# Three modulation sets of the first block, each for one vector, summed by elements on VectorE instead of multiplied on TensorE

## The chip, the cores and the metric

The kernel runs on one core of a Trainium2 chip. The metric is the time of one execution on the device in microseconds; before the change the median of three runs is 2258.77 us (2258.53 to 2259.44). The engines that matter here are TensorE (PE in the profile: matrix products and transposes), VectorE (DVE), ScalarE (ACT), GpSimd (POOL) and SyncE (SP), whose queue starts the loads of the weights by DMA.

## The reference

The program is a chain of three blocks on 256 tokens of width 1024, all in fp32: a block of attention, spatial gating and a mixture of experts; a block with a half feed-forward layer before and after a two-way recurrent mixing; and a last block. The change touches the first one, which in short is:

```python
def adaln(cvec, w_mod, b_mod):
    m = jax.nn.silu(cvec) @ w_mod + b_mod
    return jnp.split(m, 6, axis=-1)

def modulate(x, g, shift, scale):
    return rmsnorm(x, g) * (1 + scale) + shift

sh1, sc1, gt1, sh2, sc2, gt2 = [m[:, None, :] for m in adaln(c, w_mod, b_mod)]
csh1, csc1, cgt1, csh2, csc2, cgt2 = adaln(c_ctx, w_mod, b_mod)
hl = modulate(xl, g_mix, sh1, sc1)
hc = modulate(xc, g_mix, csh1, csc1)
...
xl_new = xl + gt1 * (mix_l @ w_out)
xl_new = xl_new + gt2 * expert_choice_ffn(modulate(xl_new, g_ffn, sh2, sc2), w_router, w1, w3, w2)
```

A modulation set is one of the six slices of 1024 columns of `silu(c) @ w_mod + b_mod`, where `w_mod` has 1024 x 6144 numbers, so a set reads 4 MB. The first two sets (sh1, sc1) are needed for the tokens and for the context (c and c_ctx). As the block returns only the tokens, the sets gt1, sh2 and sc2 are needed for c alone.

## The kernel before

Work on one core is put out in program order for each engine by a scheduler, which interleaves what the code writes as separate steps; the order on an engine is then fixed, and an engine whose next instruction waits does nothing else meanwhile.

*Loads.* Every weight comes in tiles of 1 MB (128 x 2048 fp32) by `load` (L253), in the order in which the code asks for them, through SyncE's queue (L258). The tiles go round a ring of buffers: six in the first block, more later. A load is issued only when the tile that had its buffer before has been used by the engine that reads it.

*Split weights.* For products of the projections a weight tile is split into a high and a low half (`halves`, L269: `wh` by ScalarE, L273, `wl` by VectorE, L274), each from a pool `hl` of five buffers per kind, and a product is three fp32r products (`mm`, L282 to L284: high x high, low x high, high x low).

*Modulation sets by products.* `ada_start` (L391) loads four tiles and does 32 products of the tile with both vectors in 32 columns (L399, tile `pa`; the profile counts 64 passes), then copies the sum out (`adaR`; L243 on ScalarE or L245 on VectorE, taking turns). `ada_end` (L406) transposes it twice on TensorE (L410, `pat`) and VectorE adds the bias (L412) into a column tile of shape 128 x 8 x 2.

*Modulation sets by elements.* `ada_one` (L419) is in the kernel already, for two sets in ffn a. VectorE multiplies each half tile by the vector's value in its partition and adds it up: one TENSOR_SCALAR (L430) and seven SCALAR_TENSOR_TENSOR (L432) of 128 x 1024 into `aacc`, from a pool `scr` of two buffers. Then TensorE adds the 128 partitions in eight products with a column of ones (L435), and VectorE adds the bias (L437).

*The order in `phase_a` (L478).* After the projections of keys, values, queries and of the gating's second half (pv), the set gt1 is started (`ada_start` of set 2), then keys are transposed (L626, `pkt`), the gating's first half u is projected (`pu`, 48 products at L282 to L284), gt1 is ended, sh2 started (set 3), queries are transposed (L638, `pqt`), and sh2 ended. Then come the scores (L689, `pS`), the softmax (L471 to L476: maximum `nm`, exponential `P` on ScalarE, reciprocal `rc`, scaling), the transposes of its result (L700, `pP`) and the values (L707, `pO`), in four pairs of heads; sc2 (set 4) stands around pair 0, a first and a second set of `w_ada` around pairs 1 and 2, with the gating between. Before the output projection (`proj_out`, products `pW`, 96 times L282 to L284, from the four tiles of `w_out`) gt1 is spread over the partitions by `bcast` (L373, `pb`). After the projection the residual is added with gt1 (L769, L770), the norm, sh2 and sc2 give the router's input (L347) and the experts' (L845, `pX`), and the experts' products begin (L874). These read 384 tiles of 1 MB; their first loads stand in SyncE's queue directly behind the last twelve tiles of `w_ada` of the first block.

Of the kernel before, what the change touches and what calls it, by code (L numbers as in the profile page):

```python
# [10 lines left out]
F32 = mybir.dt.float32  # L11
# [218 lines left out]
class Kern:  # L230
# [185 lines left out]
            op=OP.add)  # L416
        return c

    def ada_one(self, w, p, s, bias, name, eng=None):  # L419

        nc = self.nc
        eng = eng or nc.vector
        acc = self.scr.tile([128, 1024], F32, tag="scr", name="aacc")
        for kp in range(4):
            t = self.load(w[p * 4 + kp])
            for i in range(2):
                k = 2 * kp + i
                tk = t[:, i * 1024:(i + 1) * 1024]
                if k == 0:
                    eng.tensor_scalar(acc, tk, s[:, k, 0:1], None, op0=OP.mult)  # L430
                else:
                    eng.scalar_tensor_tensor(acc, tk, s[:, k, 0:1], acc, op0=OP.mult, op1=OP.add)  # L432
        ps = self.psc.tile([128, 512], F32, tag="c", name="pa1")
        for j in range(8):
            nc.tensor.matmul(ps[:, j:j + 1], acc[:, j * 128:(j + 1) * 128], self.ones[:, 0:1], start=True, stop=True)  # L435
        c = self.pers.tile([128, 8, 1], F32, name=name)
        nc.vector.tensor_tensor(c[:, :, 0], ps[:, 0:8], self.col(bias, 8 * p, 8), op=OP.add)  # L437
        return c
# [39 lines left out]
    def phase_a(self, pf_es):  # L478
        tc, nc, a = self.tc, self.nc, self.a
# [11 lines left out]
        def B8(name, dt=F32):  # L491
            return big.tile([128, 2048], dt, tag="b8", name=name)
# [3 lines left out]
        s1 = self.ada_in(("c", "c_ctx"), "s1")  # L496
# [121 lines left out]
        u = mid.tile([128, 2, 512], F32, tag="m4", name="u", bufs=5)  # L618
        for t in range(2):
            nc.scalar.activation(vv[:, t], pv[t], AF.Gelu)  # L620
        gt1R = self.ada_start(a["w_mod"], 2, s1)
        k3f = k3.rearrange("p s h r d -> p s h (r d)")
        for o in range(2):
            ps = self.psc.tile([128, 512], F32, tag="c", name="pkt")
# [1 line left out]
                nc.tensor.transpose(ps[:, s * 128:(s + 1) * 128], k3f[:, s, o], self.ident)  # L626
            self.copy(kz[:, o], ps, "av"[o])
        pu = self.by_token(wu, hl)
        gt1 = self.ada_end(gt1R, 2, "b_mod", "gt1")
        sh2R = self.ada_start(a["w_mod"], 3, s1)  # L630
        for t in range(2):
            nc.scalar.activation(u[:, t], pu[t], AF.Gelu)
        qT = mid.tile([128, 4, 256], F32, tag="m4", name="qT", bufs=5)
        for hh in range(2):
# [3 lines left out]
                    nc.tensor.transpose(ps[:, i * 256 + t * 128:i * 256 + (t + 1) * 128],  # L638
                                        qr[:, t, (2 * hh + i) * 128:(2 * hh + i + 1) * 128], self.ident)
            self.copy(qT[:, 2 * hh:2 * hh + 2], ps.rearrange("p (i n) -> p i n", i=2))  # L640
        sh2 = self.ada_end(sh2R, 3, "b_mod", "sh2")

        for t in range(2):
            sq = self.scr.tile([128, 1024], F32, tag="scr", name="sq")
# [67 lines left out]
        def pair(hp):  # L712
            for i in range(4 * hp, 4 * hp + 4, 2):
                for j in (i + 2, i + 3):
                    if j < 16:
                        scores(j)
                values(i)
                values(i + 1)
# [11 lines left out]

        scores(0)
        scores(1)
        sc2R = self.ada_start(a["w_mod"], 4, s1)
        pair(0)
        sc2 = self.ada_end(sc2R, 4, "b_mod", "sc2")
        R = self.ada_start(a["w_ada"], 0, self.s2)
        pair(1)
        self.m2[0] = self.ada_end(R, 0, "b_ada", "m2_0")
# [1 line left out]
        R = self.ada_start(a["w_ada"], 1, self.s2)  # L740
        pair(2)
        self.m2[1] = self.ada_end(R, 1, "b_ada", "m2_1")
        A2 = self.gain(sc2, self.col("g_ffn"), "A2")
        gt1b = mid.tile([128, 1024], F32, tag="m4", name="gt1b", bufs=5)
        self.bcast(gt1[:, :, 0], 8, gt1b)
        proj_out(2, True, False)
        proj_out(3, False, False)
        pair(3)
        ws = [self.load(a["w_out1"][kp]) for kp in range(2)]
        att.close()  # L750
        with self.more_ring(4, None, last=True):
            proj_out(0, False, False, ws[0])
# [22 lines left out]
        hr = B8("hr").rearrange("p (k n) -> p k n", k=8)  # L775
        self.to_T(xn2, A2[:, :, 0:1], sh2[:, :, 0:1], [hr])
        xs = [B8("xs" + p, F32R).rearrange("p (t d) -> p t d", t=2) for p in "hl"]
# [63 lines left out]
        for k in range(8):  # L841
            ps = self.psc.tile([128, 512], F32, tag="c", name="pX")
            for t in range(2):
                for i in range(2):
                    nc.tensor.matmul(ps, xs[i][:, t, k * 128:(k + 1) * 128], Pm[:, t].rearrange("p e c -> p (e c)"),  # L845
                                     start=(t == 0 and i == 0), stop=(t == 1 and i == 1))
            self.scaled(ps, A2[:, k, 0:1], sh2[:, k, 0:1], [self.xe[:, k]])

# [1096 lines left out]
```

## Time and profile before

| | before |
|---|---|
| median of three runs | 2258.77 us (2258.53 to 2259.44) |
| the profiled execution | 2256.84 us, its span 2255.0 us |
| TensorE busy | 1990.1 us, 88% of the span |
| VectorE busy | 784.2 us, 35% |
| ScalarE busy | 609.9 us, 27% |
| GpSimd busy | 99.8 us, 4% |
| moved by DMA | 666.19 MB, 295 GB/s over the span |
| mean granted TensorE clock | 0.955 |

All durations below come from the one profiled execution, which took 1.93 us less than the median of the runs. Its span runs from the first to the last instruction, and another 1.84 us lie around it. A share of the span is an average over stages that are limited by different things; the slices and the stretches in the section of rows show them apart. In a timeline a row with x16 is a group of 16 of a kind and its duration runs from the first start to the last end; the count is of passes, and one fp32 product can be two or more of them.

### The profile page before, as it was taken

The numbers are of one execution on the slowest core, as the hardware profiler recorded it, in microseconds if no ns is written. First come the engines' busy times: TensorE is split into PE (matmuls) and PEld (weight loads), VectorE is DVE, ScalarE is ACT, GpSimd is POOL, SyncE is SP. The second block draws the span as 40 slices with busy tenths as digits, with TensorE's granted clock in tenths as the row PEclk, the third lists the DMA queues.
The fourth block names the chain that finished last, engine by engine and source line by source line (L and its number), as shares of the span: only waits on it lengthen the run. The fifth ranks groups of instructions, "written<-read, shape, count | busy, mean of one in ns | idle before, by whom it ended". The sixth has DMA issues, their size and how long they took to land.

```text
span 2255.0 us, 29344 instructions
## 1 busy us (share of the span) xinstructions
PE 1990.1 (88%) x12348; PEld 1343.4 (60%) x12348; DVE 784.2 (35%) x1327; ACT 609.9 (27%) x1012; POOL 99.8 (4%) x182
## 2 busy tenths in 40 slices
PE   6998788888877888798887699989999999989997
PEld 4664334444434222243232399989889799978886
DVE  4464000000000000122011366557655555555666
ACT  4342100000000000011000244445444444445564
POOL 2200000000000000000000100010000000021030
PEclk9999899999999999999999999999999999999998
DMA  9669999999999999999999867534135655524221
GB/s 374 254 270 388 420 419 420 419 409 420 420 419 420 420 419 418 420 416 418 420 417 418 353 245 259 182 132 171 54 133 189 244 188 195 186 76 144 100 94 57
DMA packets 93268, 666.19 MB, mean 295 GB/s; under 512 B 10352, under 2 KB 10736, under 8 KB 13392
## 3 DMA queue, kind: packets, MB, share of 16 engines
q1 hardware_dynamic: 92416, 661.99, 74.1%
q8 instruction: 97, 1.59, 0.3%
q0 software_dynamic: 576, 2.10, 0.2%
q10 hardware_dynamic: 144, 0.23, 0.0%
q14 instruction: 35, 0.29, 0.0%
HBM read 663.23 MB, written 1.05 MB: 295 GB/s over the span
## 4 chain that ended last, share of the span: by engine, by line
PE 56%; DMA 25%; issue 10%; DVE 4%; ACT 3%; POOL 1%; SPq 0%; POOLq 0%; DVEq 0%; ACTq 0%
DMA w<-in_w_dram 23%; PE pu L874 7%; PE pu L1092 6%; PE py L912 4%; PE pd L1106 3%; PE pj L284 2%; PE pj L282 2%; PE pj L283 2%; PE pu L282 2%; PE pu L284 2%; PE pu L283 2%; DMA w<-in_w_mod_dram 2%; PE pl L282 1%; PE pl L284 1%; PE pl L283 1%
## 5 line engine op out<-in xcount | busy, mean ns | idle before, releaser
L874 PE MATMUL pu<-w,xe 128*32 128x512 f32 x2048 | 354.2, 668 | 97.4 <-DMA w<-in_w_dram 97.4
L274 DVE TENSOR_TENSOR wl<-w,wh 128x1024 fp32r<-128x1024 f32 (+1 forms) x286 | 348.2, 1221 | 236.2 <-ACT wh L273 236.0
L273 ACT ACTIVATE wh<-w 128x1024 fp32r<-128x1024 f32 (+1 forms) x286 | 299.5, 1053 | 329.0 <-PE pu L283 86.4
L874 PEld LDWEIGHTS pu<-w,xe 128*32 128x32 f32 x2048 | 80.9, 119 | 349.2 <-DMA w<-in_w_dram 187.9
L912 PE MATMUL py<-w,hT 128*32 128x512 f32 x1024 | 181.5, 641 | 65.6 <-DMA w<-in_w_dram 65.6
L283 PE MATMUL pu<-ul,wh 128*128 128x256 f32 x704 | 199.8, 284 | 1.1 <-DVE ul L365 1.1
L282 PE MATMUL pu<-uh,wh 128*128 128x256 f32 x704 | 200.1, 284 | 0.6 <-ACT uh L364 0.5
L284 PE MATMUL pu<-uh,wl 128*128 128x256 f32 x704 | 199.8, 284 | 0.8 <-DVE wl L274 0.8
L1092 PE MATMUL pu<-xu,w 128*128 128x256 f32 x704 | 157.8, 382 | 0.0
L912 PEld LDWEIGHTS py<-w,hT 128*32 128x32 f32 x1024 | 40.4, 115 | 195.5 <-DMA w<-in_w_dram 120.3
L1092 PEld LDWEIGHTS pu<-xu,w 128*128 128x128 f32 x704 | 131.9, 190 | 35.5 <-issue 18.4
L1097 DVE TENSOR_TENSOR xhT<-xs,pu 128x256 f32<-128x256 f32 x22 | 9.3, 421 | 381.6 <-ACT xs L1096 369.5
L283 PEld LDWEIGHTS pu<-ul,wh 128*128 128x128 f32 x704 | 135.6, 193 | 3.0 <-DVE ul L365 1.5
L282 PEld LDWEIGHTS pu<-uh,wh 128*128 128x128 f32 x704 | 135.5, 193 | 2.5 <-ACT uh L364 0.7
L284 PEld LDWEIGHTS pu<-uh,wl 128*128 128x128 f32 x704 | 135.5, 193 | 1.2 <-DVE wl L274 1.2
L1096 ACT ACTIVATE xs<-pu 128x256 f32<-128x256 f32 x22 | 8.4, 383 | 396.7 <-PE pu L1092 396.7
L284 PE MATMUL pj<-mu,wl 128*128 128x256 f32 x320 | 90.9, 285 | 4.4 <-DVE wl L274 4.4
L282 PE MATMUL pj<-mu,wh 128*128 128x256 f32 x320 | 91.0, 285 | 0.3 <-DVE val L1453 0.3
L283 PE MATMUL pj<-mu,wh 128*128 128x256 f32 x320 | 90.7, 283 | 0.0
L290 POOL TENSOR_SCALAR rs_v<-ss 128x1 f32<-128x1 f32 (+2 forms) x36 | 12.6, 351 | 1548.6 <-DVE ss L1116 690.1
L896 DVE TENSOR_TENSOR sil<-sil,pu 128x1024 f32<-128x1024 f32 x8 | 9.8, 1221 | 200.0 <-PE pu L874 200.0
L1106 PE MATMUL pd<-w,xhT 128*128 128x512 f32 x176 | 78.5, 599 | 0.0
(632 smaller groups left out, 3236.4 us busy)
## 6 DMA issues: line engine op xcount, KB each, us to landing
w<-in_w_dram SPq DMA_DIRECT2D x384, 1024.0 KB, 11.9
w<-in_w13a_dram SPq DMA_DIRECT2D x44, 1024.0 KB, 9.0
w<-in_w_ada_dram SPq DMA_DIRECT2D x36, 1024.0 KB, 7.3
w<-in_w_mod_dram SPq DMA_DIRECT2D x24, 1024.0 KB, 9.7
w<-in_w2a_dram SPq DMA_DIRECT2D x22, 1024.0 KB, 9.0
w<-in_w13b_dram SPq DMA_DIRECT2D x22, 1024.0 KB, 4.9
w<-in_w2b_dram SPq DMA_DIRECT2D x11, 1024.0 KB, 4.9
w<-in_w_out_dram SPq DMA_DIRECT2D x8, 1024.0 KB, 4.9
```

The source lines that it names most:

```text
L273: self.nc.scalar.activation(hi, v, AF.Copy)
L274: self.nc.vector.tensor_tensor(lo, v, hi.bitcast(F32), op=OP.subtract)
L282: self.nc.tensor.matmul(out, l[0], r[0], start=start, stop=False)
L283: self.nc.tensor.matmul(out, l[0], r[1], start=False, stop=False)
L284: self.nc.tensor.matmul(out, l[1], r[0], start=False, stop=stop)
L290: nc.gpsimd.tensor_scalar(v[:, :w], ss, 1.0 / n, EPS, op0=OP.mult, op1=OP.add)
L874: last = nc.tensor.matmul(ps[32 * j:32 * j + 32, n], self.xe[:, k, e * 32:(e + 1) * 32], ts[j][:, i * 1024 + n * 512:i * 1024 + (n + 1) * ...
L896: nc.vector.tensor_tensor(hid, s, p3.rearrange("p n c -> p (n c)"), op=OP.mult)
L912: last = nc.tensor.matmul(py[32 * j:32 * j + 32, n], hT[:, f, 32 * j:32 * j + 32], ts[j][:, i * 1024 + n * 512:i * 1024 + (n + 1) * 512], ...
L1092: nc.tensor.matmul(ps[:, ab * 256:(ab + 1) * 256], w[:, k * 256 + ab * 128:k * 256 + (ab + 1) * 128], uT[:, k], start=(k == 0), stop=(k == 7))
L1097: nc.vector.tensor_tensor(hT[:, f], s, ps[:, 256:], op=OP.mult)
L1106: nc.tensor.matmul(py[t][n], hT[:, f, t * 128:(t + 1) * 128], w[:, i * 1024 + n * 512:i * 1024 + (n + 1) * 512], start=(f == 0), stop=(f = ...
```

## The change

The three sets are computed by `ada_one`, through a small helper that takes the accumulator from the pool of the low halves (`wl`, five buffers) instead of `scr`. gt1 stays where it was started; sh2 moves from between the queries' transposes to behind pair 2, ahead of the spreading of gt1; sc2 and its gain A2 move from pair 0 to behind pair 3 and the loads of the last two `w_out` tiles. With the sets their loads move in SyncE's queue, where the eight first tiles of `w_ada` now come between those of gt1 and sh2, and the four of `w_out` between sh2 and sc2. The three results have one column, 128 x 8 x 1, where they had two. Three copies that took their turn between ScalarE and VectorE (`adaR`) are no longer there.

```diff
--- before.py
+++ after.py
@@ -416,11 +416,11 @@
             op=OP.add)
         return c
 
-    def ada_one(self, w, p, s, bias, name, eng=None):
+    def ada_one(self, w, p, s, bias, name, eng=None, acc=None):
 
         nc = self.nc
         eng = eng or nc.vector
-        acc = self.scr.tile([128, 1024], F32, tag="scr", name="aacc")
+        acc = self.scr.tile([128, 1024], F32, tag="scr", name="aacc") if acc is None else acc
         for kp in range(4):
             t = self.load(w[p * 4 + kp])
             for i in range(2):
@@ -618,7 +618,12 @@
         u = mid.tile([128, 2, 512], F32, tag="m4", name="u", bufs=5)
         for t in range(2):
             nc.scalar.activation(vv[:, t], pv[t], AF.Gelu)
-        gt1R = self.ada_start(a["w_mod"], 2, s1)
+
+        def one(p, name):
+            acc = self.hl.tile([128, 1024], F32, tag="wl", name="aacc")
+            return self.ada_one(a["w_mod"], p, s1, "b_mod", name, acc=acc)
+
+        gt1 = one(2, "gt1")
         k3f = k3.rearrange("p s h r d -> p s h (r d)")
         for o in range(2):
             ps = self.psc.tile([128, 512], F32, tag="c", name="pkt")
@@ -626,8 +631,6 @@
                 nc.tensor.transpose(ps[:, s * 128:(s + 1) * 128], k3f[:, s, o], self.ident)
             self.copy(kz[:, o], ps, "av"[o])
         pu = self.by_token(wu, hl)
-        gt1 = self.ada_end(gt1R, 2, "b_mod", "gt1")
-        sh2R = self.ada_start(a["w_mod"], 3, s1)
         for t in range(2):
             nc.scalar.activation(u[:, t], pu[t], AF.Gelu)
         qT = mid.tile([128, 4, 256], F32, tag="m4", name="qT", bufs=5)
@@ -638,7 +641,6 @@
                     nc.tensor.transpose(ps[:, i * 256 + t * 128:i * 256 + (t + 1) * 128],
                                         qr[:, t, (2 * hh + i) * 128:(2 * hh + i + 1) * 128], self.ident)
             self.copy(qT[:, 2 * hh:2 * hh + 2], ps.rearrange("p (i n) -> p i n", i=2))
-        sh2 = self.ada_end(sh2R, 3, "b_mod", "sh2")
 
         for t in range(2):
             sq = self.scr.tile([128, 1024], F32, tag="scr", name="sq")
@@ -730,9 +732,7 @@
 
         scores(0)
         scores(1)
-        sc2R = self.ada_start(a["w_mod"], 4, s1)
         pair(0)
-        sc2 = self.ada_end(sc2R, 4, "b_mod", "sc2")
         R = self.ada_start(a["w_ada"], 0, self.s2)
         pair(1)
         self.m2[0] = self.ada_end(R, 0, "b_ada", "m2_0")
@@ -740,13 +740,15 @@
         R = self.ada_start(a["w_ada"], 1, self.s2)
         pair(2)
         self.m2[1] = self.ada_end(R, 1, "b_ada", "m2_1")
-        A2 = self.gain(sc2, self.col("g_ffn"), "A2")
+        sh2 = one(3, "sh2")
         gt1b = mid.tile([128, 1024], F32, tag="m4", name="gt1b", bufs=5)
         self.bcast(gt1[:, :, 0], 8, gt1b)
         proj_out(2, True, False)
         proj_out(3, False, False)
         pair(3)
         ws = [self.load(a["w_out1"][kp]) for kp in range(2)]
+        sc2 = one(4, "sc2")
+        A2 = self.gain(sc2, self.col("g_ffn"), "A2")
         att.close()
         with self.more_ring(4, None, last=True):
             proj_out(0, False, False, ws[0])
```

On TensorE, behind the last products of the gating's second half (pp is pv and pu; pa_700 is gt1's sum over the partitions, pkt the keys' transposes):

```order
 L283 MATMUL pp<-wl,hlh 128x512
 L284 MATMUL pp<-wh,hll 128x512
-L399 MATMUL pa<-w,s_108 32x256 x32
-L626 MATMUL pkt<-ident,k_517 128x128 x8
+L435 MATMUL pa_700<-ones,aacc 128x1 x8
+L631 MATMUL pkt<-ident,k_517 128x128 x8
 L282 MATMUL pp<-wh,hlh 128x512
 L283 MATMUL pp<-wl,hlh 128x512
```

The 32 products of gt1 are gone, and its eight products with ones stand at the same place, ahead of the keys' transposes and of pu. On VectorE, at the same place in the program (qr is the rotated queries, vv the gating's second half, kz the transposed keys, s_108 the vector of c):

```order
 L274 TENSOR_TENSOR wl<-w,wh 128x1024
 L567 TENSOR_TENSOR qr<-rt 128x8x32
-L648 SCALAR_TENSOR_TENSOR vv<-vv,rs_r,vg 128x512 x2
+L430 TENSOR_SCALAR aacc<-w,s_108 128x1024
+L432 SCALAR_TENSOR_TENSOR aacc<-w,s_108,aacc 128x1024 x2
+L650 SCALAR_TENSOR_TENSOR vv<-vv,rs_r,vg 128x512
+L432 SCALAR_TENSOR_TENSOR aacc<-w,s_108,aacc 128x1024
+L650 SCALAR_TENSOR_TENSOR vv<-vv,rs_r,vg 128x512
+L432 SCALAR_TENSOR_TENSOR aacc<-w,s_108,aacc 128x1024 x4
+L437 TENSOR_TENSOR gt_709<-pa_700,cols 128x8
 L245 COPY kz<-pkt 128x512
-L412 TENSOR_TENSOR gt_791<-pat,cols 128x16
```

The eight element steps of gt1 stand behind the last rotation and among the two steps of vv; before, only vv stood there. On TensorE at the end of pair 2, before the change (pW_874 and pW_875 are the output projection's two halves of tokens, pb the spreading of gt1):

```order
L282 MATMUL pW_875<-wh,mixTh 128x512
L700 MATMUL pP<-ident,P 128x128 x4
L283 MATMUL pW_875<-wl,mixTh 128x512
L284 MATMUL pW_875<-wh,mixTl 128x512
L282 MATMUL pW_875<-wh,mixTh 128x512
L707 MATMUL pO<-PT,vsb 64x256
L410 MATMUL pat<-ident,adaR 128x128 x2
L707 MATMUL pO<-PT,vsb 64x256 x7
L373 MATMUL pb<-ident,gt_791 128x128 x8
L283 MATMUL pW_875<-wl,mixTh 128x512
L284 MATMUL pW_875<-wh,mixTl 128x512
```

and at the same place in the changed kernel (pW_806 and pW_807 are the same two tiles, pa_1215 is sh2's sum over the partitions):

```order
L702 MATMUL pP<-ident,P 128x128 x8
L709 MATMUL pO<-PT,vsb 64x256
L410 MATMUL pat<-ident,adaR 128x128 x2
L282 MATMUL pW_806<-wh,mixTh 128x512
L282 MATMUL pW_807<-wh,mixTh 128x512
L709 MATMUL pO<-PT,vsb 64x256 x7
L435 MATMUL pa_1215<-ones,aacc 128x1 x8
L373 MATMUL pb<-ident,gt_709 128x128 x8
L283 MATMUL pW_806<-wl,mixTh 128x512
L284 MATMUL pW_806<-wh,mixTl 128x512
```

sh2's eight products have come between the values and the spreading of gt1, and of the products pW two stand ahead of the spreading where there were ten.

## Rows read from the trace of the kernel before

**Rows 1.** The page's second part: the span in 40 equal slices of 56.4 us, each digit a tenth of busy time, and the bytes moved.

```profile
PE   6998788888877888798887699989999999989997
...
DMA  9669999999999999999999867534135655524221
GB/s 374 254 270 388 420 419 420 419 409 420 420 419 420 420 419 418 420 416 418 420 417 418 353 245 259 182 132 171 54 133 189 244 188 195 186 76 144 100 94 57
```

**Rows 2.** Busy time of the engines in two stretches of the span; columns: stretch in us, its length, busy us and instructions of each engine, granted TensorE clock, DMA share, GB/s.

```profile
172.00:1285.00 1113.00, 924.73 (x4852) 390.67 (x4850) 117.21 (x242) 73.98 (x130) 15.98 (x35) 0.94 1.01 418
161.40:171.90 10.50, 10.50 (x52) 7.48 (x52) 1.96 (x6) 2.32 (x6) 0.00 (x0) 1.00 0.01 2
```

**Rows 3.** The start of the stream of weights, from four views: the timeline of SyncE's own queue (start us, us, line, operation, count), twice; the table of what that queue waited for from 76 to 260 us (us in total, times, longest); and the chain of waits in order of time (start us, us, what), twice.

```profile
171.90 5.02 SPq L258 DMA_DIRECT2D w<-in_w_ada_dram  x6
...
216.43 2.82 SPq L258 DMA_DIRECT2D w<-in_w_dram  x4
...
SPq L258 <- PE pW L284: 17.0, 2, 15.1
...
174.67 1.04 PE pa L399 x16
...
212.85 7.12 PE pu L874 x64
```

**Rows 4.** The timeline of TensorE from 75.6 to 85 us, where the set gt1 is computed; columns: start us, us from the first start to the last end of the group, line, operation, shapes, count, and in brackets the idle time before it and what ended it.

```profile
76.18 3.66 PE L399 MATMUL pa<-w,s 128*32 128x256 f32 x64
79.77 1.09 PE L626 MATMUL pkt<-ident,k 128*128 128x128 f32 x8
...
83.91 0.52 PE L282 MATMUL pp<-wh,hlh 128*128 128x512 f32 x1 [2.35 <-ACT adaR L243]
```

**Rows 5.** The timeline of VectorE from 80 to 97 us, same columns.

```profile
82.36 0.41 DVE L567 TENSOR_TENSOR qr<-rt 128x256 f32<-128x256 f32 x1
...
84.54 0.75 DVE L648 SCALAR_TENSOR_TENSOR vv<-vv,rs_r,vg 128x512 f32<-128x512 f32 x1 [0.91 <-POOL rs_r L291]
85.21 0.68 DVE L245 COPY kz<-pkt 128x512 f32<-128x512 f32 x1
...
96.47 0.17 DVE L412 TENSOR_TENSOR gt<-pat,cols 128x16 f32<-128x16 f32 x1 [10.57 <-PE pat L410]
```

**Rows 6.** The element form of a modulation set as it already runs, in ffn a: the two lines on VectorE (shortest, median, longest in ns; first and last start), two steps back to back, and the products that add the partitions.

```profile
L430 DVE TENSOR_SCALAR aacc<-w,s x2: 750/752/753, 1305.6 to 1373.4; 128x1024 f32<-128x1024 f32 x2
...
L432 DVE SCALAR_TENSOR_TENSOR aacc<-w,s,aacc x14: 1280/1284/1285, 1308.0 to 1397.3; 128x1024 f32<-128x1024 f32 x14
...
1310.71 2.61 DVE L432 SCALAR_TENSOR_TENSOR aacc<-w,s,aacc 128x1024 f32<-128x1024 f32 x2 [0.26 <-DMA w<-in_w_ada_dram]
...
1332.95 1.84 PE L435 MATMUL pa<-ones,aacc 128*128 128x1 f32 x16
```

**Rows 7.** Busy time of the engines in the 2 us after the wait at 83.91, columns as in rows 2.

```profile
84.00:86.00 2.00, 2.00 (x6) 1.56 (x7) 1.35 (x2) 0.34 (x1) 0.92 (x2) 0.56 0.77 307
```

**Rows 8.** The timeline of TensorE from 95 to 108 us, from the end of pu to the first attention weights.

```profile
96.05 0.38 PE L410 MATMUL pat<-ident,adaR 128*128 128x128 f32 x2
96.36 3.66 PE L399 MATMUL pa<-w,s 128*32 128x256 f32 x64
99.95 1.09 PE L638 MATMUL pqt<-ident,qr 128*128 128x128 f32 x8
100.88 0.38 PE L410 MATMUL pat<-ident,adaR 128*128 128x128 f32 x2
101.29 1.13 PE L689 MATMUL pS<-kz,qT 64*128 64x512 f32 x4
102.35 3.66 PE L399 MATMUL pa<-w,s 128*32 128x256 f32 x64
...
107.00 1.09 PE L700 MATMUL pP<-ident,P 128*128 128x128 f32 x8
```

**Rows 9.** The timeline of VectorE from 102 to 106 us, the first softmax.

```profile
102.45 1.29 DVE L471 TENSOR_REDUCE nm<-pS 128x1 f32<-128x512 f32 x2 [0.60 <-PE pS L689]
103.99 0.16 DVE L475 RECIPROCAL rc<-sm 128x1 f32<-128x1 f32 x1 [0.25 <-ACT P L473]
104.19 0.49 DVE L476 TENSOR_SCALAR P<-P,rc 128x512 f32<-128x512 f32 x1
```

**Rows 10.** Busy time of the engines in two stretches of the attention and output projection, columns as in rows 2, and a low half of a split weight on VectorE in the first of them.

```profile
127.84:145.98 18.14, 17.82 (x141) 10.50 (x142) 15.34 (x33) 11.05 (x20) 0.00 (x0) 1.00 0.71 284
146.32:166.09 19.77, 19.10 (x101) 13.70 (x100) 9.69 (x18) 7.49 (x14) 0.00 (x0) 1.00 0.53 184
...
135.67 1.23 DVE L274 TENSOR_TENSOR wl<-w,wh 128x1024 fp32r<-128x1024 f32 x1 [0.26 <-ACT wh L273]
```

**Rows 11.** Single pieces of the timelines of TensorE and VectorE in the same stretches and of TensorE near the end of the output projection.

```profile
145.87 2.05 PE L373 MATMUL pb<-ident,gt 128*128 128x128 f32 x16
...
145.98 0.42 DVE L245 COPY mxv<-pO 128x256 f32<-128x256 f32 x1 [0.56 <-PE pO L707]
...
160.25 0.52 PE L700 MATMUL pP<-ident,P 128*128 128x128 f32 x3 [0.67 <-DVE P L476]
...
172.17 0.40 PE L284 MATMUL pW<-wh,mixTl 128*128 128x512 f32 x1
172.41 0.40 PE L282 MATMUL pW<-wh,mixTh 128*128 128x512 f32 x1
```

## The prediction

> **What bounds the kernel now.** I read the page's slices first. From the fifth slice to the twenty-second (each is 56.4 us) the DMA engines are busy nine tenths or more of the time at about 419 GB/s, while TensorE stands at 7 to 9 [rows 1]. The stretch table gives it as one row: from 172 to 1285 us the DMA share is 1.01 at 418 GB/s, and TensorE is busy 924.73 of 1113 us [rows 2]. So for 1113 us the weight stream sets the pace, a tile of 1 MB each 2.5 us (1.0486 MB by 418 GB/s). Behind it the slices turn to TensorE at 9.
>
> The reader should then ask what starts that stream, since whatever delays its start delays all behind it. From 161.4 to 171.9 us the DMA share is 0.01 [rows 2]. SyncE's own queue issues the next tile at 171.90 and the table of its waits names the attention output's products (pW, L284), 17.0 us in two waits [rows 3]. The first product of the next block (pa) stands in the chain at 174.67, where pW has ended [rows 3]; with 0.24 us from product to product (172.17 to 172.41 [rows 11]) the release is about the twelfth product before the end. The experts' products begin at 212.85 and release the next tiles at 216.43 [rows 3], far inside the stream. My reading: **a microsecond by which pW ends later is a microsecond of the whole**, since the stream neither has spare rate to catch up nor anything else to wait for.
>
> So the question is when pW ends, and the three modulation sets all stand in front of it. There TensorE is the busy engine: 17.82 of 18.14 and 19.10 of 19.77 us in two stretches [rows 10].
>
> **Costs of one set.** Before, a set is 32 products in 64 passes, 3.66 us [rows 4], and two transposes, 0.31 to 0.41 us from start to start (96.05 to 96.36, 100.88 to 101.29 [rows 8]). The new form is already in the kernel, elsewhere: one step L430 of 0.752 us, seven steps L432 of 1.284 us, two of them back to back 2.61 us, so 1.33 from start to start [rows 6]. A set is 0.79 + 7 x 1.33 = 10.1 us of VectorE. Then eight products of one column in 16 passes, 1.84 us on TensorE [rows 6], which need the finished sum. The three sets thus take 3 x (3.66 + 0.4) = 12.2 us from TensorE, give it 5.5, and give VectorE 30 us. What counts is whether VectorE has them done when TensorE comes to them.
>
> The Trainium skill, "VectorE: DVE Perf Modes", its section on the errata and the fixed latency per instruction, puts an fp32 tensor_tensor at (N + 151) / 0.96 ns, 1.22 us for 1024 elements. For the sum taken as such an instruction a set would be 0.4 us shorter; the rows of L432 itself show 1.284, so the measurement decides and I keep 10.1.
>
> **First set (gt1).** In the changed order the eight products of the sum stand on TensorE directly behind the last pv product and ahead of the key transposes (pkt) and all 48 pu products; VectorE's eight steps stand behind the last rotation (qr), with the two vv steps between. The last qr ends at 82.36 + 0.41 = 82.8; a vv step is 0.67 from start to start (84.54 to 85.21) [rows 5]. So the sum is ready at 82.8 + 10.1 + 2 x 0.67 = 94.2, and with 1.84 for the products and 0.1 for the handing over pkt begins at 96.1 in place of 79.77 [rows 4]: +16.3. That is idle TensorE, since everything behind is queued in order. Before, pu stood still 2.35 us at 83.91 for a high half that ScalarE made behind the set's copy [rows 4]; that half will long be there: -2.35. In the 2 us after that wait the granted clock was 0.56, nearly all of it the lower of the two levels, 1.2 GHz [rows 7]. After the longer wait I expect the same kind of stretch, now under the eight products and pkt, and count it at nothing against the one that goes; if it comes on top it costs up to 1.8 us (the products at half speed).
>
> The Trainium skill, "TensorE: Matmul & The Clock Gate", Part 1, says an idle TensorE falls to its half rate and must be busy again before it returns. The row at 84 agrees. By that rule the new idle time ends in one such stretch, as the old one did, so the sum is the same and only the upper end has the 1.8.
>
> End of pu: +14.0 (96.05 becomes 110.0).
>
> **Up to the first attention output.** Gone between pu and the scores are gt1's transposes (0.31), sh2's products (96.36 to 99.95, 3.59) and its transposes (0.41) [rows 8]: -4.3, +9.7 at the first pS. sc2's products (3.59, 102.35) go too, but they covered the softmax. Before, pP began 107.00 - 101.29 = 5.71 us after the first pS. Now four pS stand in a row, VectorE does four maxima of 0.61 from 1.16 us after the first pS (102.45, two in 1.29) and then reciprocal and scaling (0.16 and 0.49, [rows 9]): 1.16 + 2.44 + 0.7 = 4.3. So only 1.4 of the 3.59 comes out: +8.3 at pP. (Bounds: +6.1 if all of it came out, +9.7 if none.) sc2's transposes, 0.4 us, go a little later: **+7.9**.
>
> **Second set (sh2).** Its steps now lie among the gating and softmax steps of pair 2, and its products stand between the last pO of the pair and pb, the spreading of gt1. In the stretch up to the copy of that pO (127.84 to 145.98) VectorE is busy 15.34 of 18.14 us [rows 10], so 2.8 are free. Four wl steps of 1.22 (first at 135.67) move behind: 4.9 free. All steps but the last stand in this stretch, 0.79 + 6 x 1.33 = 8.8; the rest of them, 1.1 us, is lateness of softmax and so of TensorE. The last step stands behind the copy of pO (0.42, 145.98 [rows 11]): 0.42 + 1.33, and 1.84 for the products, before pb can begin. Together 4.7, pb at +12.6. Also, before ten of the products pW (L282 to L284) stood ahead of pb, filling waits, now two: 8 x 0.24 = 1.9 still to be done behind it, **+14.5**. Bounds for the 4.7: 1.84 if all steps hide and the products alone count; 10.1 + 0.42 + 1.84 = 12.4 if none hides.
>
> The loads move as well: sh2's four tiles now come behind the eight of w_ada, sc2's behind four of w_out. In both stretches the DMA share is 0.71 and 0.53 [rows 10], so there is rate for them. A slot is free only when the tile six places earlier is used, though, so sh2's third tile waits for the second w_ada set's first: VectorE may stand up to a tile's 2.5 us. I count 0 and keep 2.5 for the upper end.
>
> **Third set (sc2).** From 146.32 to 166.09 VectorE is busy 9.69 of 19.77 us [rows 10]: 10.1 free, just the set, though 4.9 of wl have come in; but by now it has 7 us more before the end of pW. In the changed order 18 products pW (4.3 us) stand behind the sum's products. So the steps cost nothing as I count, the products 1.84, and pair 3's wait of 0.67 at 160.25 [rows 11] is lost in it: +1.2. Uncovered it would be up to 5 more: the last four steps (5.3 us) stand behind a wl step that waits for pW to free its buffer.
>
> **Sum.** +7.9 + 4.7 + 1.9 + 1.2 = +15.7 at the end of pW, and by the reading above at the end of the kernel. The profiled execution took 2256.84 us (span 2255.0), so 2272.5 for its like; the median of the runs, 2258.77, lies 1.9 above it, so **2274.5 us**. Three copies fewer flip the turn of ScalarE and VectorE in every later alternating copy; the order of TensorE and SyncE is otherwise nearly the same, and I take 0, with 2 us either way.
>
> **Rivals.**
> *The later two sets hide* (0.20). Only the first wait counts, as the second and third sets' steps fit in VectorE's waits and the pW products fill TensorE's: +7.9 + 2 x 1.84 - 0.67 = +10.9, 2269.7. For it: VectorE is off the critical path in most rows there. Against it: 15.34 of 18.14 us are taken before pb. With the softmax bound (-2.2) it reaches 2267.5.
> *The third set, or sh2's tiles, hold TensorE too* (0.15): +15.7 + 5, 2279.5. For it: the wl steps in between and the ring; against it: 4.3 us of pW behind the products and 7 us more time.
> *TensorE is not held* (0.04), the other side: if VectorE had the sums ready before TensorE needs them, the change takes 12.2 - 5.5 = 6.7 us from TensorE, and the 2.35 us wait: -9.0, 2249.8. It decides at one point: the first sum must be done by 76.2, where pv ends. VectorE's queue has its steps behind a qr that ends at 82.8; only tiles and steps far earlier could do it. Its idle 10.57 us before 96.47 [rows 5] come too late for that.
> *The stream absorbs it* (0.05): the delay ends in slack and the time stays 2258.8. Against it stands the DMA share of 1.01 over 1113 us.
> The forecast has 0.56, with a range of its own from 2270 to 2278.
>
> What a measurement of this kernel can tell from no change is about 0.2%, 4.5 us. All but the last two cases are slower by more: faster 0.04, same 0.05, slower 0.91. The range of 8 in 10 reaches from the hidden case's lower end past the upper rival: 2266.5 to 2280.5.
>
> **What the profile after should show.** TensorE idle some 18 us from 76 until the sum's products near 94, waiting for L432; pu's end at 110; pb 12 to 13 us later than 145.87 [rows 11], behind a wait for L432; pW's end at 190 to 191; SyncE's restart with it, 12 products earlier, near 188; the DMA share at 1.01 from there to about 1301. I am wrong if TensorE's wait at 76 is under 10 us, if pW ends before 185 or after 197, or if the end of the DMA-bound stretch doesn't move by as much as its start.

## The result, and the profile after

The changed kernel takes 2274.57 us (median of four runs, 2269.97 to 2277.01) against 2259.11 us of the kernel before on the same chip (four runs): ratio 1.0068, 95% interval 1.0053 to 1.0083. It is slower by 15.5 us where 15.7 were forecast, and its median lies within a tenth of a microsecond of the forecast 2274.5; the sum behind the forecast is not that exact, as is shown below. The profiled execution took 2275.43 us, its span is 2273.7 us, 18.7 longer than before.

The page's slices after, which answer [rows 1]:

```profile
PE   6688788888888888888888699999999999989997
...
DMA  9468999999999999999999966544235655523221
GB/s 370 149 250 360 420 420 421 421 408 421 421 420 421 421 417 421 421 420 420 417 420 420 398 233 227 210 143 167 73 114 199 244 188 193 188 74 130 97 109 56
```

The stream of weights is as wide and as long as before; it stands later. The timeline of TensorE at the first set, which answers [rows 4, 8] (start us, us, instruction, idle time before and what ended it):

```profile
94.62 3.54 PE L435 MATMUL pa<-ones,aacc 128*128 128x1 f32 x16 [17.61 <-DVE aacc L432]
98.02 1.95 PE L631 MATMUL pkt<-ident,k 128*128 128x128 f32 x8
...
112.12 1.04 PE L641 MATMUL pqt<-ident,qr 128*128 128x128 f32 x8
113.46 1.99 PE L691 MATMUL pS<-kz,qT 64*128 64x512 f32 x8 [0.30 <-ACT qT L243]
117.84 1.22 PE L702 MATMUL pP<-ident,P 128*128 128x128 f32 x8 [2.40 <-DVE rc L475]
```

The reader should see the 17.61 us in which TensorE waits for the last step of gt1's sum, and then products that take 3.54 us where [rows 6] had 1.84. The granted clock explains the latter (stretches as in [rows 7]); it is 0.50, the lower of its two levels, from 94 to 102:

```profile
94.00:96.00 2.00, 1.38 (x7) 1.41 (x7) 0.47 (x1) 0.00 (x0) 0.00 (x0) 0.50 1.10 436
...
100.00:102.00 2.00, 2.00 (x6) 1.52 (x6) 0.69 (x1) 0.00 (x0) 0.00 (x0) 0.50 0.00 0
102.00:112.00 10.00, 10.00 (x44) 8.04 (x43) 0.00 (x0) 0.37 (x1) 0.00 (x0) 0.98 0.00 0
```

VectorE at the same place, which answers [rows 5]: the steps follow the last rotation without a gap.

```profile
83.08 0.41 DVE L567 TENSOR_TENSOR qr<-rt 128x256 f32<-128x256 f32 x1
83.41 0.74 DVE L430 TENSOR_SCALAR aacc<-w,s 128x1024 f32<-128x1024 f32 x1
...
89.23 5.24 DVE L432 SCALAR_TENSOR_TENSOR aacc<-w,s,aacc 128x1024 f32<-128x1024 f32 x4
```

At the end of pair 2 TensorE waits for a scaling that stands behind sh2's steps on VectorE, and then for the sum itself, and the granted clock from 150 to 160 is 0.83; pb begins 16.2 us later than in [rows 11]. The timeline, and the stretch:

```profile
152.24 1.07 PE L702 MATMUL pP<-ident,P 128*128 128x128 f32 x8 [1.93 <-DVE P L476]
...
160.26 1.95 PE L435 MATMUL pa<-ones,aacc 128*128 128x1 f32 x16 [1.71 <-DVE aacc L432]
162.07 2.03 PE L373 MATMUL pb<-ident,gt 128*128 128x128 f32 x16
```

```profile
150.00:160.00 10.00, 6.38 (x29) 3.14 (x28) 8.48 (x17) 6.62 (x12) 0.00 (x0) 0.83 1.01 424
```

SyncE's restart, which answers [rows 3]; there are seven tiles of w_ada behind it where there were six:

```profile
190.82 5.41 SPq L258 DMA_DIRECT2D w<-in_w_ada_dram  x7
196.38 1.19 SPq L258 DMA_DIRECT2D w<-in_w_dram  x2
```

The end of the stream (stretches) and the first product of ffn a behind it, after and then before; both stand 20 us later:

```profile
1295.00:1300.00 5.00, 3.15 (x7) 0.89 (x6) 4.05 (x6) 1.37 (x3) 0.63 (x2) 1.00 1.01 418
1300.00:1305.00 5.00, 0.00 (x0) 0.00 (x0) 4.28 (x4) 4.74 (x7) 2.74 (x5) 0.54 0.96 385
```

```profile
1306.01 1.65 PE L335 MATMUL pt<-diag,x 128*128 128x128 f32 x6 [7.86 <-DVE diag L314]
```

```profile
1280.00:1285.00 5.00, 0.00 (x0) 0.00 (x0) 4.28 (x4) 4.74 (x7) 2.75 (x5) 0.73 0.98 382
...
1286.19 1.19 PE L335 MATMUL pt<-diag,x 128*128 128x128 f32 x4 [7.95 <-DVE diag L314]
```

### The profile page after: what moved, and what is told of

The parts are those of the page before. It is cut to its first block, busy times and chain, and to the rows that moved or that the text cites. A ratio compares the mean times of both kernels' runs of the same rounds, so it can differ in the third digit from the quotient of the medians.

```text
span 2273.7 us, 29083 instructions
## 1 busy us (share of the span) xinstructions
PE 1992.5 (88%) x12198; PEld 1345.9 (59%) x12198; DVE 810.2 (36%) x1349; ACT 609.6 (27%) x1011; POOL 101.2 (4%) x182
## 4 chain that ended last, share of the span: by engine, by line
PE 52%; DMA 28%; issue 10%; DVE 5%; ACT 3%; POOL 2%; SPq 0%; POOLq 0%; DVEq 0%; ACTq 0%
DMA w<-in_w_dram 25%; PE pu L876 6%; PE pu L1094 6%; PE py L914 4%; PE pd L1108 3%; PE pj L284 2%; PE pj L282 2%; PE pj L283 2%; PE pu L284 2%; PE pu L282 2%; PE pu L283 2%; DMA w<-in_w_mod_dram 2%; PE pl L283 1%; PE pl L284 1%; PE pl L282 1%
## 5 line engine op out<-in xcount | busy, mean ns | idle before, releaser
L284 PE MATMUL pu<-uh,wl 128*128 128x256 f32 x704 | 199.2, 283 | 1.5 <-DVE wl L274 1.5
L284 PEld LDWEIGHTS pu<-uh,wl 128*128 128x128 f32 x704 | 134.7, 192 | 2.1 <-DVE wl L274 2.1
L284 PE MATMUL pj<-mu,wl 128*128 128x256 f32 x320 | 90.7, 283 | 2.0 <-DVE wl L274 2.0
```

What stands on the lines that cost most here:

```text
L284: self.nc.tensor.matmul(out, l[1], r[0], start=False, stop=stop)
```

## The experiments

For reading them together: the medians, and of each profiled execution, in us of its span, the first scores, the first gating product, the end of the last pW (its start and 0.24), the landing of the first tile of the experts, the start of ffn a, and the span. A profiled execution is one run; it can lie several us from its median (2 under it before, 6 under in e2, 9 above in e5). From ffn a to the end, where the kernels have the same products on TensorE, the profiled executions take 960.5 (e2) to 972.7 us (e6), so the last column does not follow from the one before it.

| kernel | median | pS | pG | pW ends | tile lands | ffn a | span |
|---|---|---|---|---|---|---|---|
| before | 2259.1 to 2259.8 | 101.3 | 127.7 | 174.5 | 193.0 | 1286.2 | 2255.0 |
| changed | 2274.57 | 113.5 | 138.3 | 193.4 | 214.5 | 1306.0 | 2273.7 |
| e1 gt1 alone | 2269.96 | 116.1 | 143.0 | 189.9 | 207.2 | 1298.9 | 2267.4 |
| e2 sh2 alone | 2258.93 | 99.2 | 125.3 | 180.5 | 197.9 | 1290.8 | 2251.3 |
| e3 sc2 alone | 2253.35 | 102.1 | 126.3 | 175.1 | 192.6 | 1285.1 | 2251.5 |
| e4 gt1's products behind pu | 2263.97 | 100.6 | 127.2 | 186.6 | 207.8 | 1299.1 | 2265.9 |
| e5 behind pair 1 | 2259.89 | 91.1 | 124.6 | 183.9 | 204.7 | 1296.6 | 2267.1 |
| e6 and sh2 by products | 2260.45 | 96.6 | 124.4 | 177.3 | 196.0 | 1287.8 | 2260.5 |
| e7 places alone | 2264.15 | 97.5 | 121.7 | 177.5 | 197.2 | 1291.7 | 2264.1 |
| e8 turns flipped | 2256.67 | 102.0 | 128.5 | 175.5 | 194.1 | 1287.3 | 2255.2 |
| e9 wait filled | 2274.76 | 112.3 | 137.6 | 194.1 | 215.1 | 1307.1 | 2273.6 |
| e10 all products late | 2261.29 | 90.3 | 122.4 | 179.2 | 202.6 | 1293.4 | 2261.1 |
| e11 sh2 beside pu | 2260.37 | 97.5 | 125.0 | 177.2 | 195.7 | 1286.3 | 2254.4 |
| e12 before, one-column products | 2266.43 | 102.0 | 131.8 | 182.1 | 200.8 | 1293.4 | 2262.1 |

The theories: A, TensorE's queue stands still behind the sums, gt1's above all; B, VectorE's added load as such; C, the moved loads and the ring.

**One set at a time (e1, e2, e3).** The other two sets stay as they were; of e3's edit against the changed kernel, the part on sh2:

```diff
+        sh2R = self.ada_start(a["w_mod"], 3, s1)
...
+        sh2 = self.ada_end(sh2R, 3, "b_mod", "sh2")
...
-        sh2 = one(3, "sh2")
```

> Only gt1 by elements, sh2 and sc2 by products at their old places. Theory A (TensorE's queue stands still until VectorE has gt1's sum): the end of pu comes about 15 us later and nothing behind takes it back, so +13 to +16 us, 2272 to 2275. Theory B (VectorE's 30 us more of work are what counts, each set bringing about a third): +5, about 2264. Theory C (the moved loads and the ring): gt1's loads do not move, so 0 to +2, about 2260.

> Only sh2 by elements, behind pair 2; gt1 and sc2 by products at their old places. Theory A: -4.0 us of TensorE ahead of the scores, about +7 to +8 ahead of and behind pb (lateness of softmax, last step, products, pW left behind pb), so +2 to +4, 2261 to 2263. Theory B: +5, about 2264. Theory C: sh2's loads stand behind eight tiles of w_ada, so this one brings most of the time, +8 or more, 2267 and up.

> Only sc2 by elements, behind pair 3; gt1 and sh2 by products at their old places. Theory A: the softmax behind the first scores loses its cover, so 1.4 us out and 0.4 of transposes, and 1.2 in near the end of pW: -2 to +1 us, 2257 to 2260. Theory B: +5, about 2264. Theory C: sc2's loads stand late, directly ahead of the stream of experts' weights: +4 or more.

Measured: e1 ratio 1.0045 (1.0031 to 1.0058), +10.7 us; e2 0.9995 (0.9983 to 1.0007); e3 0.9971 (0.9959 to 0.9983), -6.0. B falls: the same 10 us of VectorE cost 10.7, nothing and less than nothing by where they stand. C falls as the chief cause, since gt1's loads don't move. A has the order right, but all three lie below its ranges (2272 to 2275, 2261 to 2263, 2257 to 2260); the flip of turns, which each of them has and e8 measures, is part of that. In e1's trace the end of pW is 15.4 us later, as A has it, and ffn a 12.7. In e2's trace the end of pW is 6.0 us later and ffn a 4.6, so its zero is not a zero in the first block. The three differences add up to 4.3 of the 15.5 us: the sets cost more together than alone. By an estimate from rows shown below some 8 of these 11 us have a name: the flip, 2.9 us, is in each of the three and only once in the changed kernel, and the seventh tile of w_ada at the release, 2.6 us, comes only there.

**gt1's products later (e4, e5).** The sum stays where it was; its products and bias, split off as `one_end`, are written further down (e4's edit against the changed kernel):

```diff
-        gt1 = one(2, "gt1")
+        gt1a = one(2, "gt1", True)
...
         pu = self.by_token(wu, hl)
+        gt1 = self.one_end(gt1a, 2, "b_mod", "gt1")
```

> The changed kernel, with the eight products and the bias of gt1 written behind pu, so that VectorE's eight steps lie beside pu's 48 products; all else as in the changed kernel. Theory A: the wait of 17.6 us and the slow clock behind it go, and pb and the end of pW come 17 to 20 us earlier than in the changed kernel: 2254 to 2258. Theory B: VectorE has the same work, so most of the loss stays: 2267 to 2273. Theory C: the loads are the same, so the loss stays.

Measured 2263.97 (1.0025, 1.0011 to 1.0038): 10.6 us come back, not 17 to 20, and A's range (2254 to 2258) is missed. The wait had moved, not gone; TensorE is through with pu before the sum is there, and the slow clock follows again:

```profile
95.34 3.54 PE L439 MATMUL pa<-ones,aacc 128*128 128x1 f32 x16 [6.08 <-DVE aacc L432]
98.74 1.95 PE L646 MATMUL pqt<-ident,qr 128*128 128x128 f32 x8
```

In e5 the products stand behind pair 1.

> All three by elements as in the changed kernel, but gt1's eight products and bias written behind pair 1. In the kernel before this one (products behind pu) TensorE still stood 6.08 us and then ran the products and the queries' transposes at half speed, 2.5 us too long. Theory A (what counts is where TensorE has to wait for the sum): these go, so 4 to 8 us below the 2264 of that kernel, 2256 to 2260; the first scores still wait for the queries' copy on VectorE behind the sum, near 96 to 98 us. Theory B (VectorE's load): no change, about 2264.

Measured 2259.89 (1.0008, 0.9995 to 1.0021), ten runs from 2255.08 to 2268.89: as A had it, at its upper end. The three sets by elements now cost nothing that can be told from the kernel before. The profiled execution is the longest of the ten, 9 us above the median, so its points in the table stand for that one. What remains of the first set's wait is 3.44 us, for a copy that VectorE makes behind the sum:

```profile
96.51 1.78 PE L695 MATMUL pS<-kz,qT 64*128 64x512 f32 x2 [3.44 <-DVE qT L245]
```

**Search for a faster mix (e6, e11).** e6 is e5 with sh2 by products at its old place. e11 has gt1 by products as before, sh2's sum beside pu and its products behind pair 1, sc2 by elements.

> gt1's sum on VectorE with its products behind pair 1, sc2 by elements behind pair 3, sh2 by products at its old place. Theory A: TensorE never waits for gt1's sum, sh2's products cover it, and a set of products (3.6 us) and the wait of 2.35 in pu go, 1.84 come: 3 to 5 us below the kernel with sc2 alone, 2248 to 2251, faster than before. Theory B: 20 us more on VectorE, so slower than the kernel with sc2 alone, 2256 or more.

> gt1 by products as before (they cover VectorE's rotations), sh2 by elements with its sum beside pu, where VectorE stood idle 10.57 us before, and its products behind pair 1; sc2 by elements behind pair 3. TensorE loses 4.0 us ahead of the first scores and gets 1.84 back later, and the scores wait for the queries' copy behind the sum by some 1 us: 1 to 3 us below the kernel with sc2 alone (2253.4), 2250 to 2253, faster than before by 6 to 9 us. If VectorE's load counts: 2256 or more.

Measured 2260.45 (1.0003, 0.9993 to 1.0012) and 2260.37 (1.0004, 0.9994 to 1.0013): both miss. The gain ahead of the scores is there (4.7 and 3.8 us), and it is gone at the end of pW (2.8 and 2.7 us late). e6's trace shows a reason; the timeline of TensorE (products of gt1 among the values of pair 1, of sc2 among those of pair 3) and three stretches:

```profile
119.06 1.72 PE L439 MATMUL pa<-ones,aacc 128*128 128x1 f32 x14
120.71 2.85 PE L715 MATMUL pO<-PT,vsb 128*64 128x256 f32 x14
...
163.50 1.95 PE L439 MATMUL pa<-ones,aacc 128*128 128x1 f32 x16
165.95 3.62 PE L715 MATMUL pO<-PT,vsb 128*64 128x256 f32 x14
```

```profile
120.00:121.00 1.00, 1.00 (x12) 0.91 (x13) 0.01 (x1) 0.00 (x0) 0.00 (x0) 1.00 0.99 418
...
122.00:123.00 1.00, 1.00 (x6) 0.46 (x2) 0.00 (x0) 0.00 (x0) 0.00 (x0) 0.50 0.06 25
...
125.00:126.00 1.00, 1.00 (x11) 1.00 (x10) 0.37 (x2) 1.00 (x2) 0.00 (x0) 1.00 0.00 0
```

TensorE is busy without a break, at the first place from 118.48 on, and yet the clock falls to the lower level behind the one-column products; the values take 2.85 and 3.62 us where e3 has 1.94 behind sc2's products:

```profile
163.72 1.95 PE L435 MATMUL pa<-ones,aacc 128*128 128x1 f32 x16
...
165.93 1.94 PE L712 MATMUL pO<-PT,vsb 128*64 128x256 f32 x14
```

Behind a wait of 2.11 us, at 137.85, there is another such fall (0.66 from 138 to 140, 0.50 from 140 to 142). e11's trace has the same at the first of these places (values of 3.54 us) and behind a wait of 1.98 us at 138.05, but 1.94 us for the values of pair 3. And two sets by elements leave the turn of ScalarE and VectorE as it was, so that the 2.5 us of e8 are missing against e3, from which I had reckoned.

**Places and loads alone (e7).** All sets by products, sh2 and sc2 at the new places; of its edit against the changed kernel (gt1 goes back to products too):

```diff
-        sh2 = one(3, "sh2")
+        sh2 = self.ada(a["w_mod"], 3, s1, "b_mod", "sh2")
...
-        sc2 = one(4, "sc2")
+        sc2 = self.ada(a["w_mod"], 4, s1, "b_mod", "sc2")
```

> All three sets by products on TensorE, but sh2 and sc2 at the places, and so with the order of loads, of the changed kernel. If the element form is what costs (A and B): sc2's products no longer cover the first softmax, +2 to +4, 2261 to 2263, and six tiles of w_ada behind the release as before. If the moved loads are what costs (C): seven or more tiles behind the release and +8 or more, 2267 and up.

Measured 2264.15 (1.0019, 1.0010 to 1.0028), +5.0: a little above what the lost cover of the softmax was to cost, below C; six tiles stand behind the release. Moving the two sets costs this much without any change of their form.

**The flipped turns (e8).**

```diff
         sc2 = self.ada_end(sc2R, 4, "b_mod", "sc2")
+        self.n_ev += 1
```

> The kernel before with the turn of ScalarE and VectorE flipped once behind pair 0, as three copies fewer do it, and nothing else. If the flip explains why the kernels with one set by elements end 2 to 5 us earlier than their first block says: 2254 to 2257. If it does nothing: 2259, within 2 us.

Measured 2256.67 (0.9984, 0.9974 to 0.9993): by the medians the flip alone gives 2.5 us (1.6 to 5.9 by the interval). Every kernel with one or three sets by elements has it; e6 and e11, with two, have not. The traces show where it gains. Behind ffn a the products of TensorE are the same in all 14 kernels, in the same number, so they can be laid side by side. In a stretch of products pj (L284), from 1514 to 1543 us in the kernel before, TensorE has one long wait there, and two short ones in e8:

```profile
1524.51 0.46 PE L284 MATMUL pj<-mu,wl 128*128 128x256 f32 x1 [3.83 <-DVE wl L274]
```

```profile
1527.53 0.39 PE L284 MATMUL pj<-mu,wl 128*128 128x256 f32 x1 [1.23 <-DVE wl L274]
...
1535.79 0.39 PE L284 MATMUL pj<-mu,wl 128*128 128x256 f32 x1 [0.77 <-DVE wl L274]
```

The same 200 passes around them take 29.3 us before and 26.4 in e8, 2.9 less. All nine kernels with the flip have 26.4 us and the two short waits; the five without (before, e6, e7, e11, e12) have 29.3 to 30.4 and the long one. That e8's profiled span is no shorter than the one before has another reason, told in the last section.

**The wait filled (e9).**

```diff
+        pj = self.psc.tile([128, 512], F32, tag="c", name="junk")
+        for j in range(144):
+            nc.tensor.transpose(pj[:, j % 4 * 128:j % 4 * 128 + 128], self.ident, self.ident)
         gt1 = one(2, "gt1")
```

> The changed kernel with 144 transposes of the identity written ahead of gt1's eight products; their result is not used, they only fill TensorE's wait of 17.6 us (some 16 us). If the clock at half speed behind that wait costs what its rows say (the products 3.54 in place of 1.84 us, the keys' transposes 1.95 in place of 1.09, the first pu products 0.43 in place of 0.23 apart): these at full speed, the end of pu 2.5 to 3.5 us earlier against the end of the sum, and 2271 to 2273. If the clock doesn't hang on the wait: no change, 2274 to 2275.

Measured 2274.76 (1.0066, 1.0051 to 1.0081): no gain, where 2271 to 2273 were expected if the clock behind the wait counts. The timeline and two stretches:

```profile
95.43 2.08 PE L435 MATMUL pa<-ones,aacc 128*128 128x1 f32 x16 [1.95 <-DVE aacc L432]
97.37 1.95 PE L634 MATMUL pkt<-ident,k 128*128 128x128 f32 x8
```

```profile
97.00:101.00 4.00, 4.00 (x18) 3.62 (x18) 0.86 (x2) 0.60 (x1) 0.00 (x0) 0.57 0.61 252
160.00:165.00 5.00, 5.00 (x31) 4.81 (x31) 3.20 (x5) 1.54 (x2) 0.00 (x0) 0.69 1.07 405
```

The sum's products run at nearly full speed, and from the first of them to pqt it is 15.5 us where it was 17.5. But behind a wait of 1.95 us and these products there is a slow stretch again, shorter than the old one, and another one came at 160, where the changed kernel has 1.00; at the end of pW the 2 us are gone. So the clock's part in the first set is 2 us of its trace; that it is 2 us of the time is not shown.

**All products late (e10).** e5, with sh2's products behind pair 3 as well, by the same edit as in e4.

> As the kernel with gt1's products behind pair 1, and sh2's products and bias written behind pair 3 too, so that no sum's products stand ahead of the spreading of gt1. If TensorE's wait for sh2's sum (1.71 us), its products at half speed (3.08) and the clock behind it are what pair 2 costs: 4 to 7 us below that kernel's 2259.9, 2253 to 2256. If it is the softmax standing behind the sum's steps on VectorE: within 2 us of 2259.9.

Measured 2261.29 (1.0000, 0.9988 to 1.0013): no gain over e5. pb comes at 139.75, 6 us before its old time, as no sum stands ahead of it any more (half of it now stands ahead of the last values of the pair); but the end of pW is 4.7 us late and the first tile of the experts 9.7, as eight tiles of w_ada now stand behind the release:

```profile
174.81 7.86 SPq L258 DMA_DIRECT2D w<-in_w_ada_dram  x8
182.77 6.54 SPq L258 DMA_DIRECT2D w<-in_w_dram  x4
```

Against e5's trace the end of pW comes 4.7 us earlier and the tile 2.0: more than half of what TensorE won there, the ring took back. Why the median shows nothing of the rest is open, as e5's trace is of its longest run.

**One-column products by themselves (e12).** In the kernel before, behind pairs 1, 2 and 3 (`pj` is a tile whose content is not used):

```diff
+            for j in range(8):
+                nc.tensor.matmul(pj[:, j:j + 1], self.ident, self.ones[:, 0:1], start=True, stop=True)
```

> The kernel before with eight products of the identity with a column of ones, of the same form as the sums' products, behind each of the pairs 1, 2 and 3; they wait for no sum, their result is not used, and VectorE and the loads are as before. If such products cost only their own time: 3 x 1.84 = 5.5 us more at the end of the products pW, the granted clock 1.00 behind them, 2264 to 2265. If the clock falls behind them although TensorE is busy, as in the kernel with gt1's products behind pair 1: 0.5 to 0.66 over some 3.5 us behind at least one of the three, and 1.7 us more for each, 2266 to 2270.

Measured 2266.43 (1.0030, 1.0020 to 1.0040), +6.6, at the lower end of the range for a falling clock. TensorE behind pair 1 and pair 2, and a stretch behind the first:

```profile
126.16 1.95 PE L736 MATMUL junk<-ones,ident 128*128 128x1 f32 x16
...
128.42 3.20 PE L707 MATMUL pO<-PT,vsb 128*64 128x256 f32 x14
...
147.72 1.95 PE L736 MATMUL junk<-ones,ident 128*128 128x1 f32 x16
...
149.76 1.94 PE L707 MATMUL pO<-PT,vsb 128*64 128x256 f32 x14
```

```profile
129.50:131.50 2.00, 2.00 (x8) 0.72 (x6) 0.00 (x0) 0.00 (x0) 0.00 (x0) 0.50 0.11 45
```

Behind the first group the clock falls, behind the other two it does not (the third, not shown, has 1.94 us too). The end of pW is 7.6 us late, ffn a 7.2, the span 7.1. Of the 7.6 us 5.5 are the products' own time and 1.3 the slower values.

## Why the prediction was right, and where its sum was not

**The stream carries a delay through.** This held, and e12 shows it best, because nothing else is changed: 7.6 us at pW's end, 7.2 at ffn a, +6.6 in the medians. In the 14 traces ffn a begins 1090.6 to 1094.5 us after the first experts' tile has landed (1093.2 before); of a delay of 10 to 22 us the stream took back 1.2 to 2.5, so "neither has spare rate to catch up" was nearly, not wholly, true.

**First set.** TensorE's wait was foreseen within half a microsecond: sum ready at 94.2, measured 94.62; some 18 us idle, measured 17.61. 0.8 us was there already when pv ended (77.0 against 76.2), before anything that was changed; over the 14 executions that point lies anywhere from 75.8 to 77.8 where it can be read. The step that failed is the clock: I counted the slow stretch at nothing against the old one, with 1.8 us as the upper end; it lasted from 94.6 to 102 and cost the products 1.7 us, the transposes 0.8 and the first products of pu 1.3, where the old one had cost pu 1.6. The end of pu came at 112.1, not 110.0. The Trainium skill, "TensorE: Matmul & The Clock Gate", Part 1, has an idle TensorE fall to half its rate; the trace agrees (0.50 behind 17.61 us of waiting). That the new stretch would be as long as the old one was my reading, and it was twice as long (94.6 to 102 against 84 to 87.7). That the wait is what counts is shown by e4 and e5: with 6.08 us of it left 10.6 us come back, with the products out of its way 14.7.

**Softmax.** From the first pS to pP 4.38 us (117.84 - 113.46) against 5.71: 1.3 out where 1.4 was forecast. Between pu and pG the shift fell from 16.1 to 10.5, by 5.6; the terms were 4.3, 1.4 and 0.4.

**Second set.** pb moved from +10.5 at pG to +16.2, 5.7, against 4.7. The two waits (1.93 and 1.71 us) and the clock of 0.83 around them are what the trace shows there; their shares were not separated. The bound of 12.4 was far off.

**Third set and the pW left behind.** 16.2 to 18.9, 2.7 against 3.1.

**A term that was missing.** I saw the ring only as a possible wait of VectorE, 2.5 us at the upper end, and not as an order of tiles at the release. With sh2 and sc2 both moved and by elements, one tile more stands behind it (seven for six; e4, e5 and e9, which have both, show seven too), and the first experts' tile lands 21.5 us late, 2.6 more than pW's end. Neither set alone shows it (e2 and e3: six), nor do the two moved as products (e7: six).

**A term at its bound.** The flip of turns was put at 0 with 2 us either way. It is worth -2.5 by e8's medians and -2.9 in the stretch of pj.

**So the sum.** By the profiled executions the change costs 18.6 us (2275.43 - 2256.84), not 15.7: 0.8 from before pv's end, 1.8 more up to pG, 1.0 more in the second set, 0.4 less in the third, 2.6 for the tile, and then 1.7 less along the stream and 1.1 less behind it. That 1.1 is itself a balance: the flip gives 2.9, a fall of the clock in the last block, which only the later of the two executions has, costs 4.4 (last section), and 2.6 less are not traced. The signs that the prediction named came three to four us late all along: pb +16.2 for 12 to 13, pW's end 193.4 for 190 to 191, the restart 190.8 for 188, the stream's end near 1305 for 1301; none passes its limit for being wrong. By the medians it is 15.5: the execution profiled before lies 2.3 us under the median of its runs, the one after 0.9 above. The mechanism and the place were right; that the median came out within 0.1 us is chance, as the terms that were put too low are made up by the flip and by how the profiled executions lie among their runs.

**The rivals.** That the later sets hide is wrong for the whole (they move pW by 8.4 us behind pG), though sh2 alone costs nothing in its median. That TensorE is held in the third set is wrong; the tile at the release has about half its price. The other two are ruled out by 17.61 us of waiting and by the 20 us that the stream's end moved. That the sums take buffers of the low halves was not tried by itself; in the changed kernel TensorE waits for no low half between 76 and 196 us.

**A version that beats both.** sc2 alone by elements: 2253.35, 6 us under the kernel before and 21 under the changed one. Part of it is the flip (2256.67); whether it beats the flip alone by more than the runs' spread was not tried side by side.

## What to carry to other kernels

Work that is moved to an idle engine is paid by whoever stands in order behind its result: ask where the first use stands in the other engine's queue, and put it as far down as the result allows (here 14.7 us, e5 against the change). A mean share of 35% says nothing of that; the ten microseconds cost 10.7 us, none or less in three places. And what holds the ring's slots at the release of a bandwidth-bound stream is part of the path, even where the engines gain.

## What was not expected of the hardware

TensorE's clock fell to the lower level while it was busy without a break: behind 14 and 16 passes of one column, the values at 0.50 (e6 at 122, e12 at 129.5), at a loss of 0.9 to 1.7 us each; yet not each time, as the other two groups in e12, the second in e11 and the one in e3 show. The Trainium skill, "TensorE: Matmul & The Clock Gate", Part 1, speaks of an idle engine; these rows show a fall without idling. Falls stand behind short waits too, 1.95 and 2.11 us, in e9 and e6.

Such falls come in one trace and not in another even where the kernels have the same instructions on TensorE. In the last block it waits twice for GpSimd, 5 us in all, and runs the same products behind that in every kernel; the stretch from the end of the first of these waits, before and in e8:

```profile
2024.60:2048.00 23.40, 20.88 (x165) 20.72 (x165) 10.16 (x18) 8.19 (x12) 1.99 (x2) 1.00 0.36 124
```

```profile
2022.40:2049.00 26.60, 24.02 (x165) 23.71 (x166) 10.29 (x18) 8.19 (x12) 2.02 (x3) 0.87 0.32 110
```

Four of the 14 profiled executions (before, e2, e11, e12) have 23.4 us at a clock of 1.00, four 26.5 at 0.87, six 27.5 to 27.8 at 0.83, with the flip and without it. This hides the flip's gain in e8's trace, and it is of the size of the differences between several of the kernels here. It fits the spread of e5 and e10 (14 and 10 us over ten runs): e5's longest run has the lowest mean clock, 0.943, but its shortest has 0.948 and not the highest, so that the falls make the spread is not shown; of each kernel only one execution was profiled.
